# Squares of chunk 1 summed by TensorE tile by tile, and the keys of chunk 0 between the memory keys and the spread of chunk 1's norm

## The chip, the cores and the metric

One core of a Trainium2 chip runs the whole program. The metric is the device time of one execution in microseconds (us); the time of a kernel is the median of its runs. Engines are named as in the profile: PE is TensorE (its weight loads are listed as PEld), DVE is VectorE, ACT is ScalarE, POOL is GpSimd, SP is SyncE, which issues nearly all DMAs here.

## What is computed

One step of a hybrid encoder layer on 1024 prompt tokens and 32 sample tokens (1056 columns, model width 1024), all in float32. Cut to what matters here:

```python
def rmsnorm(x, g):
    x32 = x.astype(jnp.float32)
    y = x32 * lax.rsqrt(jnp.mean(x32 * x32, axis=-1, keepdims=True) + EPS)
    return (y * g.astype(jnp.float32)).astype(x.dtype)

def memory_kv(mem, g, wk, wv):
    mn = rmsnorm(mem, g)
    mk = (mn @ wk).reshape(B, M, X_HEADS, X_HEAD_DIM)
    mv = (mn @ wv).reshape(B, M, X_HEADS, X_HEAD_DIM)

q, k, v, ga, bb, cc, hh, gb, xq, gx, mg = split(rmsnorm(x, g) @ w_in)
# window attention (q, k, v), short convolution (cc, hh, bb), attention into 256 memory tokens (xq, mk, mv),
# each times its SiLU gate and projected; the three merged, projected by w_out, added to x; a last rmsnorm
```

The change lies in the head of the program: the norm of x, the memory keys and values, and the first projections (keys and values, then queries).

## The kernel before

x lies transposed, width on the partitions: two chunks of 528 columns (c = 0, 1), each in eight tiles of 128 x 528, two to a buffer (`xr`). The work of the head, for each chunk:

- ACT squares the eight tiles (`sq`, tag `gt`, three buffers); DVE adds them into the first one (`x_squares`, L461); TensorE then sums that one tile over its 128 partitions with six small matmuls against a column of ones (`csx`, L417, in `column_rstd`).
- DVE turns the sums into mean + eps (`vax`, L421), POOL raises them to the power -0.5 (`rsx`, L424).
- TensorE spreads the result over the partitions with six more matmuls (`rpx`, L428, in `r_chunk`), ACT copies that out (`Rx`, L436), and DVE multiplies the eight tiles by it (L466, `x_norm`).
- ACT and DVE split each normed piece into a high part (`xh`, `b`, L483) and a low part (`xl`, `b`, L95), the operands of all later products (`x_blocks`); `x_sums` makes further operands from sums of pieces (`kwt`, `qht`, `aot`, `vwt`, L500), which are first used by the group q2 behind the queries.

Every float32 product is three matmuls (high by high, high by low, low by high: L99, L100, L101, in `mm3`). `kv_group` makes keys and values from the operands of a chunk (`pdkv`): it is a generator, and each `next(kv)` emits the work up to its next yield. `q_direct` makes the first queries in four passes (`pdq`): weight tile 0 for chunk 0 and chunk 1, then weight tile 1 for chunk 0 and chunk 1. Its weights, too, are split by ACT (`whq`, L115) and DVE (`wlq`, L95). `mk_step(f)`, f = 0 to 3, makes the memory keys (`mkp`, L585), eight float32 matmuls each, which the trace records as two each.

Each engine runs its instructions in the order in which they stand in the program; a framework of tiles sets the semaphores, gives buffers out, and may move an instruction against the order of the code. All input loads stand in one row on SP. From the group q2 on, POOL prepares the weights of the long middle of the program (`S_q`, L131, and `wlq`, L95).

Of the kernel before, what the change touches and what calls it, by code (L numbers as in the profile page):

```python
# [33 lines left out]
def stream_kernel(tc, A, O):  # L34
# [4 lines left out]
    with ExitStack() as ctx:  # L39
# [333 lines left out]
        def kv_group(nm, f2):  # L373
# [3 lines left out]
            for c in range(2):  # L377
                for i in range(2):
                    ps = bank2(f"pd{nm}{c}{i}")
                    for s in range(2):  # L380
                        for kh in range(2):
                            hi, lo = w[2 * i + kh]
                            for k in range(4):
                                kc = slice(k * 128, (k + 1) * 128)
                                xh, xl = (x[k] for x in XD[c, kh, s])
                                mm3(ps[:, s, :H], hi[:, kc], lo[:, kc], xh, xl, kh + k == 0, kh == 1 and k == 3)
                    act.copy(o[i].rearrange("p (s c h) -> p s c h", s=2, c=2)[:, :, c], ps[:, :, :H])
                if c == 0:
                    yield
            yield  # L390
# [21 lines left out]
        def column_rstd(parts, cols, w, nm, pair_=False):  # L412

            ps = bank2(f"cs{nm}")[:, 0] if pair_ else bank(f"cs{nm}")
            for j in range(cols):
# [24 lines left out]
        def slot(c, j, l):  # L440
            return 14 * c + 2 * j + l
# [11 lines left out]
        def x_squares(c):  # L453
# [8 lines left out]
            return tot  # L462

# [433 lines left out]
        for i in range(4):  # L897
            if i < 3:
                mem_load(i + 1)
            for k in (2 * i, 2 * i + 1):  # L900
                wmv.append(mem_w(A["w_mv"][k], f"rmv{k}", ("whi", "wlo")[k // 4], 4))
                if 0 < k < 5:
                    x_load(0, k - 1, slot(1, (T1, T2)[(k - 1) // 2], (k - 1) % 2))
        for k in range(4):
            x_load(1, k, slot(1, (T4, T3)[k // 2], k % 2))
        wmk = [mem_w(A["w_mk"][k], f"rmk{k}", *(("S", 3), ("qh", 2), ("kw", 2), ("vw", 2), ("ao", 2), ("raw", 5))[max(k - 2, 0)])
               for k in range(8)]
# [4 lines left out]
        sq = [x_squares(c) for c in range(2)]  # L912
        r0 = column_rstd([sq[0]], 6, 88, "x0", True)
        MS["rs"] = column_rstd([MS["acc"][:, :256], MS["acc"][:, 256:]], 2, 128, "m", True)
        mk_step(0)
        R0 = r_chunk(r0, "x0")
        x_norm(0, R0)
        mk_step(1)
        r1 = column_rstd([sq[1]], 6, 88, "x1", True)
# [3 lines left out]
        mk_step(3)  # L923
        R1 = r_chunk(r1, "x1")
# [5 lines left out]
        x_blocks(1, [sb.tile([128, NT], F32R, name=f"b12c1{l}", tag="O", bufs=4) for l in range(2)])  # L930
        next(kv)
# [284 lines left out]
```

## Time and profile before

| | us |
|---|---|
| median of 3 runs | 1005.92 (1005.43 to 1006.57) |
| the profiled execution, its own time | 1011.11 |
| its span, first to last instruction | 1009.3 |
| PE busy in the span | 982.1 |
| DVE, ACT, POOL busy in the span | 510.7, 465.1, 561.4 |

The rows are times within the one profiled execution, counted from its first instruction. A busy engine is one with an instruction under way; what it waits for in a given stretch is read from that stretch and not from the share of the whole span.

### The profile page before, as it was taken

Reading aid. Unit: us, or ns where it says so; the run is one execution under the profiler, and the core shown is the slowest. Engines: PE = TensorE matmul, PEld = TensorE weight load, DVE = VectorE, ACT = ScalarE, POOL = GpSimd, SP = SyncE. Lnnn points to the kernel's source line nnn. Section 1 sums busy time; section 2 is a strip of 40 time slices with the busy share of each in tenths; the row PEclk is TensorE's granted clock in tenths of the full one; section 3 lists DMA queues with packets and bytes.
Section 4 is the critical chain, followed back from the end, with each engine's and each line's share of the span. In section 5 each row is a group of like instructions: output and inputs, shape, how many; then the busy total and the mean of one; then the engine's idle time right before and its main releaser. Section 6 shows DMA issues by size and latency. Waiting matters only on the chain.

```text
span 1009.3 us, 20193 instructions
## 1 busy us (share of the span) xinstructions
PE 982.1 (97%) x7887; PEld 958.1 (95%) x7887; DVE 510.7 (51%) x836; ACT 465.1 (46%) x969; POOL 561.4 (56%) x422
## 2 busy tenths in 40 slices
PE   8799999999999999999999999999999999999996
PEld 4699999999999999999999999999999999999996
DVE  3787333466575656565443333333374472552464
ACT  5454434455445454454454545545372242243452
POOL 0505677665667676767555555555554444444463
PEclk9899999999999999999999999999999999999998
DMA  9445633454423232322354444434686678653473
GB/s 338 145 150 156 204 133 110 152 170 138 128 67 103 74 112 85 99 75 86 105 161 149 154 151 148 138 120 153 210 281 201 182 201 254 183 188 88 126 233 118
DMA packets 115711, 153.06 MB, mean 152 GB/s; under 512 B 14400, under 2 KB 73888, under 8 KB 115616
## 3 DMA queue, kind: packets, MB, share of 16 engines
q1 hardware_dynamic: 115040, 151.24, 48.0%
q8 instruction: 62, 1.02, 0.4%
q10 hardware_dynamic: 576, 0.54, 0.2%
q14 instruction: 33, 0.27, 0.1%
HBM read 109.49 MB, written 42.25 MB: 150 GB/s over the span
## 4 chain that ended last, share of the span: by engine, by line
PE 85%; DVE 8%; DMA 2%; ACT 2%; POOL 2%; issue 1%; SPq 0%; POOLq 0%; DVEq 0%; ACTq 0%
PE y L99 4%; PE y L101 4%; PE y L100 4%; PE wo L99 3%; PE wo L101 3%; PE wo L100 3%; PE pamg L99 2%; PE pamg L100 2%; PE pdmg L99 2%; PE pamg L101 2%; PE pdmg L100 2%; PE pdmg L101 2%; PE pcmg L99 2%; PE pcmg L100 2%; PE pcmg L101 2%; PE mvp L550 2%
## 5 line engine op out<-in xcount | busy, mean ns | idle before, releaser
L95 POOL TENSOR_TENSOR wlp<-rp,whp 128x512 fp32r<-128x512 f32 x80 | 104.9, 1312 | 128.7 <-ACT whp L115 128.6
L115 ACT CAST whp<-rp 128x512 fp32r<-128x512 f32 x96 | 59.6, 621 | 130.3 <-PE y L100 78.7
L99 PE MATMUL y<-br,whp 128*128 128x264 f32 x384 | 109.2, 284 | 1.2 <-DVE z L271 1.2
L100 PE MATMUL y<-br,whp 128*128 128x264 f32 x384 | 109.1, 284 | 0.0
L101 PE MATMUL y<-br,wlp 128*128 128x264 f32 x384 | 109.0, 284 | 0.0
L95 POOL TENSOR_TENSOR wlmg<-S_mg,whmg 128x512 fp32r<-128x512 f32 x48 | 62.7, 1307 | 56.2 <-ACT whmg L115 42.5
L95 POOL TENSOR_TENSOR wlmg<-rmg,whmg 128x512 fp32r<-128x512 f32 x36 | 47.0, 1306 | 62.1 <-ACT whmg L115 59.3
L101 PE MATMUL wo<-zo,wlp 128*128 128x264 f32 x256 | 73.0, 285 | 0.8 <-POOL wlp L95 0.8
L99 PE MATMUL wo<-zo,whp 128*128 128x264 f32 x256 | 73.2, 286 | 0.3 <-ACT whp L115 0.3
L99 PEld LDWEIGHTS y<-br,whp 128*128 128x128 f32 x384 | 72.1, 188 | 1.3 <-ACT whp L115 1.3
L100 PE MATMUL wo<-zo,whp 128*128 128x264 f32 x256 | 72.6, 284 | 0.0
L100 PEld LDWEIGHTS y<-br,whp 128*128 128x128 f32 x384 | 72.3, 188 | 0.0
L101 PEld LDWEIGHTS y<-br,wlp 128*128 128x128 f32 x384 | 72.3, 188 | 0.0
L99 PE MATMUL pcmg<-xh,whmg 128*128 128x264 f32 x192 | 55.5, 289 | 1.2 <-DVE omg L218 1.2
L99 PE MATMUL pamg<-xh,whmg 128*128 128x264 f32 x192 | 55.3, 288 | 0.0
L99 PE MATMUL pdmg<-xh,whmg 128*128 128x264 f32 x192 | 55.2, 287 | 0.0
L100 PE MATMUL pcmg<-xl,whmg 128*128 128x264 f32 x192 | 54.7, 285 | 0.0
L100 PE MATMUL pdmg<-xl,whmg 128*128 128x264 f32 x192 | 54.7, 285 | 0.0
L100 PE MATMUL pamg<-xl,whmg 128*128 128x264 f32 x192 | 54.7, 285 | 0.0
L101 PE MATMUL pdmg<-xh,wlmg 128*128 128x264 f32 x192 | 54.6, 284 | 0.0
L101 PE MATMUL pcmg<-xh,wlmg 128*128 128x264 f32 x192 | 54.4, 284 | 0.0
L101 PE MATMUL pamg<-xh,wlmg 128*128 128x264 f32 x192 | 54.4, 283 | 0.0
(493 smaller groups left out, 3674.3 us busy)
## 6 DMA issues: line engine op xcount, KB each, us to landing
MGd<-omg SPq DMA_DIRECT2D x24, 528.0 KB, 3.6
sg<-MGd SPq DMA_DIRECT2D x48, 264.0 KB, 3.1
rmg<-in_w_in SPq DMA_DIRECT2D x48, 256.0 KB, 2.8
rp<-in_w_p SPq DMA_DIRECT2D x48, 256.0 KB, 3.1
rp<-in_w_out SPq DMA_DIRECT2D x48, 256.0 KB, 2.8
xr<-in_xT SPq DMA_DIRECT2D x8, 528.0 KB, 7.9
res<-in_xT SPq DMA_DIRECT2D x8, 528.0 KB, 5.7
qtw<-Qd SPq DMA_DIRECT2D x32, 128.0 KB, 2.6
```

What stands on the lines that cost most here:

```text
L95: eng.tensor_tensor(out=lo, in0=x, in1=hi.bitcast(F32), op=ALU.subtract)
L99: pe.matmul(out, lh, rh, start=first, stop=False, skip_group_check=free)
L100: pe.matmul(out, lh, rl, start=False, stop=False, skip_group_check=free)
L101: pe.matmul(out, ll, rh, start=False, stop=last, skip_group_check=free)
L115: act.copy(hi, src)
L550: pe.matmul(mps[m], mt(k)[:, m * 128:(m + 1) * 128], w, start=k == 0, stop=k == 7)
```

## The change

It changes four things, all in the head. Chunk 1's squares are no longer added up by DVE: a new function `x_columns` lets TensorE sum each of the eight squared tiles by itself, with six matmuls each that add into the same bank, and the main row calls it in pieces (four tiles, two tiles, two tiles) between the steps of the memory keys. The first two loads of `w_mk` are issued between the two halves of chunk 1. `kv_group` yields also after the keys of a chunk, and its first part (the keys of chunk 0) is called ahead of `r_chunk` for chunk 1. The squares of chunk 1 are called behind both statistics of chunk 0 and of the memory.

```diff
                     act.copy(o[i].rearrange("p (s c h) -> p s c h", s=2, c=2)[:, :, c], ps[:, :, :H])
-                if c == 0:
                     yield
-            yield
             move(out=O["attn_k"], in_=o[0][:, 896:1056])
...
-        def column_rstd(parts, cols, w, nm, pair_=False):
-
-            ps = bank2(f"cs{nm}")[:, 0] if pair_ else bank(f"cs{nm}")
-            for j in range(cols):
+        def column_rstd(parts, cols, w, nm, pair_=False, sums=None):
+
+            ps = sums if sums is not None else bank2(f"cs{nm}")[:, 0] if pair_ else bank(f"cs{nm}")
+            for j in range(cols if sums is None else 0):
...
+        def x_columns(c, ks, st={}):
+
+            if 0 in ks:
+                st["ps"] = bank2(f"csx{c}")[:, 0]
+            for k in ks:
+                sq_ = half("gt", f"sq{c}_{k}", F32, 3)
+                act.activation(sq_, xk(c, k), AF.Square)
+                for j in range(6):
+                    pe.matmul(st["ps"][:88, 2 * j:2 * j + 2], sq_[:, j * 88:(j + 1) * 88], one.broadcast_to([128, 2]),
+                              start=k + j == 0, stop=k == 7 and j == 5, skip_group_check=True)
+            return st["ps"]
...
         for k in range(4):
+            if k == 2:
+                wmk_load(0)
+                wmk_load(1)
             x_load(1, k, slot(1, (T4, T3)[k // 2], k % 2))
...
-        sq = [x_squares(c) for c in range(2)]
-        r0 = column_rstd([sq[0]], 6, 88, "x0", True)
+        r0 = column_rstd([x_squares(0)], 6, 88, "x0", True)
         MS["rs"] = column_rstd([MS["acc"][:, :256], MS["acc"][:, 256:]], 2, 128, "m", True)
+        x_columns(1, range(4))
         mk_step(0)
+        x_columns(1, range(4, 6))
         R0 = r_chunk(r0, "x0")
         x_norm(0, R0)
         mk_step(1)
-        r1 = column_rstd([sq[1]], 6, 88, "x1", True)
+        r1 = column_rstd(None, 6, 88, "x1", sums=x_columns(1, range(6, 8)))
         x_blocks(0, [xslot(slot(0, T4, l), f"b12{l}", F32R) for l in range(2)])
         kv = kv_group("kv", (T_K, T_V))
         mk_step(2)
         mk_step(3)
+        next(kv)
         R1 = r_chunk(r1, "x1")
         x_norm(1, R1)
         mem_spread()
...
+        next(kv)
         next(kv)
         x_sums(0)
```

What this does to the order on the engines is shown at three places. Numbers behind a name tell buffers apart and differ between the two programs. The first is PE from the column sums of chunk 0 (`csx0`) on. Before, the spread of chunk 0 (`rpx0`) follows them, then the memory keys of steps 0 and 1 (`mkp0`), and the column sums of chunk 1 (`csx1`) behind these:

```order
L417 MATMUL csx0_235<-cst_81,sq0_0_189 88x2 x6
L428 MATMUL rpx0_264<-cst_81,rsx0_244 128x88 x6
L585 MATMUL mkp0_255<-memt0_96,rmk0_136 128x256 x2
L585 MATMUL mkp0_255<-memt1_98,rmk0_136 128x256 x2
L585 MATMUL mkp0_255<-memt2_106,rmk1_138 128x256 x2
L585 MATMUL mkp0_255<-memt3_116,rmk1_138 128x256 x2
L585 MATMUL mkp0_255<-memt0_96,rmk2_140 128x256 x2
L585 MATMUL mkp0_255<-memt1_98,rmk2_140 128x256 x2
L585 MATMUL mkp0_255<-memt2_106,rmk3_142 128x256 x2
L585 MATMUL mkp0_255<-memt3_116,rmk3_142 128x256 x2
L417 MATMUL csx1_289<-cst_81,sq1_0_212 88x2 x6
```

Of the change, the same place, behind the column sums of chunk 0 and down to its spread (`mkp0` down to `rmk1` is step 0):

```order
L470 MATMUL csx1_232<-cst_81,sq1_0_233 88x2 x6
L470 MATMUL csx1_232<-cst_81,sq1_1_241 88x2 x6
L595 MATMUL mkp0_265<-memt0_96,rmk0_132 128x256
L470 MATMUL csx1_232<-cst_81,sq1_2_249 88x2 x6
L595 MATMUL mkp0_265<-memt0_96,rmk0_132 128x256
L470 MATMUL csx1_232<-cst_81,sq1_3_257 88x2 x6
L595 MATMUL mkp0_265<-memt1_98,rmk0_132 128x256 x2
L595 MATMUL mkp0_265<-memt2_106,rmk1_134 128x256 x2
L595 MATMUL mkp0_265<-memt3_116,rmk1_134 128x256 x2
L470 MATMUL csx1_232<-cst_81,sq1_4_274 88x2 x6
L470 MATMUL csx1_232<-cst_81,sq1_5_282 88x2 x6
L426 MATMUL rpx0_290<-cst_81,rsx0_221 128x88 x6
```

Six groups of column sums and the whole of step 0 now stand ahead of chunk 0's spread; the last two groups stand behind step 1. Of the keys of chunk 0 the framework puts only two matmuls ahead of chunk 1's spread; the spread is third in the row behind step 3.

The second place is DVE between `vax1` (chunk 1's mean) and the multiplications by chunk 1's norm (L466). Before, its end is:

```order
L95 TENSOR_TENSOR wlkv10_396<-rkv10_393,whkv10_395 128x512
L95 TENSOR_TENSOR wlkv11_402<-rkv11_399,whkv11_401 128x512
L500 TENSOR_TENSOR kwt00_649<-xr0_0_104 128x528
L500 TENSOR_TENSOR kwt01_650<-xr0_1_110 128x528
L500 TENSOR_TENSOR qht00_651<-xr0_2_114,kwt00_649 128x528
L500 TENSOR_TENSOR qht01_652<-xr0_3_120,kwt01_650 128x528
L95 TENSOR_TENSOR xl0_3_654<-kwt00_649,xh0_3_653 128x528
L466 SCALAR_TENSOR_TENSOR xr1_0_128<-xr1_0_128,cst_81,Rx1_348 128x528 x2
```

Of the change:

```order
L95 TENSOR_TENSOR wlkv10_391<-rkv10_388,whkv10_390 128x512
L95 TENSOR_TENSOR wlkv11_397<-rkv11_394,whkv11_396 128x512
L476 SCALAR_TENSOR_TENSOR xr1_0_128<-xr1_0_128,cst_81,Rx1_459 128x528 x2
L476 SCALAR_TENSOR_TENSOR xr1_1_130<-xr1_1_130,cst_81,Rx1_459 128x528 x2
L476 SCALAR_TENSOR_TENSOR xr1_2_136<-xr1_2_136,cst_81,Rx1_459 128x528 x2
```

The five subtractions of `x_sums` (`kwt`, `qht`, `xl0_3`) that stood ahead of chunk 1's norm now stand behind it, among the pieces of chunk 1.

The third place is DVE around `wlq010`, the low part of the weights of the queries' third pass. Before, from the last piece `xl1_4` (chunk 1) on:

```order
L95 TENSOR_TENSOR xl1_4_777<-xr1_1_130,xh1_4_776 128x528
L367 SCALAR_TENSOR_TENSOR q1q000_747<-pdq000_697,q0q000_746 128x528
L95 TENSOR_TENSOR xl1_6_783<-aot10_752,xh1_6_782 128x528
L95 TENSOR_TENSOR xl1_6_783<-aot11_753,xh1_6_782 128x528
L95 TENSOR_TENSOR wlq010_854<-rq010_851,whq010_853 128x512
```

Of the change:

```order
L367 SCALAR_TENSOR_TENSOR q1q000_782<-pdq000_732,q0q000_781 128x528
L510 TENSOR_TENSOR xr1_1_130<-xr1_3_138,xr1_1_130 128x2x264
L510 TENSOR_TENSOR aot11_788<-xr1_3_138,vwt11_790 128x528
L277 SCALAR_TENSOR_TENSOR e1kv0_881<-okv_0_400,e0kv0_880 128x528
L95 TENSOR_TENSOR xl1_4_812<-xr1_0_128,xh1_4_811 128x528
L95 TENSOR_TENSOR xl1_4_812<-xr1_1_130,xh1_4_811 128x528
L95 TENSOR_TENSOR wlq010_889<-rq010_886,whq010_888 128x512
```

Between `q1q000` (the low part of the first queries, the first instruction in a long row with only one input from SBUF, the other from PSUM) and `wlq010` there stood two instructions; now there are five. From the first L466 of chunk 1 to `wlq010` there stood 51, and now 54.

## Rows read from the trace of the kernel before

**Rows 1.** Busy time on the page: engine, us, share of span, instructions.

```profile
PE 982.1 (97%) x7887; PEld 958.1 (95%) x7887; DVE 510.7 (51%) x836; ACT 465.1 (46%) x969; POOL 561.4 (56%) x422
```

**Rows 2.** Busy time by stretch: start:end, length, engines, granted clock, DMA share, GB/s.

```profile
24.82:26.94 2.12, 0.00 (x1) 0.00 (x1) 1.88 (x5) 1.28 (x2) 1.84 (x2) 1.00 1.05 387
27.70:31.00 3.30, 3.30 (x13) 2.94 (x12) 1.14 (x2) 1.67 (x3) 0.18 (x1) 0.50 1.04 372
45.00:48.00 3.00, 0.00 (x0) 0.00 (x0) 2.76 (x5) 1.25 (x2) 3.00 (x1) 1.00 0.85 265
48.20:54.90 6.70, 5.91 (x26) 5.85 (x27) 2.38 (x4) 2.57 (x5) 0.73 (x1) 0.50 0.06 23
100.00:1009.00 909.00, 892.69 (x7345) 880.68 (x7344) 441.01 (x732) 414.03 (x879) 534.57 (x410) 1.00 0.48 147
```

**Rows 3.** Waits of PE in the first 75 us: total, times, longest.

```profile
PE rpx L428 <- POOL rsx L424: 6.1, 2, 4.0
```

**Rows 4.** Timeline of PE in the head: start, us, instruction, [idle before <- releaser].

```profile
23.79 1.03 PE L417 MATMUL csx<-cst,sq 128*88 128x2 f32 x12
26.94 2.25 PE L428 MATMUL rpx<-cst,rsx 88*128 88x88 f32 x12 [2.12 <-POOL rsx L424]
36.95 1.03 PE L417 MATMUL csx<-cst,sq 128*88 128x2 f32 x12
37.84 7.15 PE L585 MATMUL mkp<-memt,rmk 128*128 128x256 f32 x32
48.99 2.86 PE L428 MATMUL rpx<-cst,rsx 88*128 88x88 f32 x12 [4.00 <-POOL rsx L424]
...
76.98 0.28 PE L99 MATMUL pdq<-xh,whq 128*128 128x264 f32 x1
...
89.52 0.39 PE L101 MATMUL pdq<-xh,wlq 128*128 128x264 f32 x1 [0.50 <-DVE wlq L95]
```

**Rows 5.** Timeline of ACT, two places.

```profile
24.86 0.64 ACT L457 ACTIVATE sq<-xr 128x528 f32<-128x528 f32 x1 [1.66 <-PE csx L417]
...
29.23 0.60 ACT L436 COPY Rx<-rpx 128x528 f32<-128x528 f32 x1 [2.85 <-PE rpx L428]
```

**Rows 6.** Timeline of DVE, from chunk 0's norm to the queries' weights.

```profile
29.86 0.77 DVE L466 SCALAR_TENSOR_TENSOR xr<-xr,cst,Rx 128x528 f32<-128x528 f32 x1 [2.53 <-ACT Rx L436]
...
38.39 0.15 DVE L421 TENSOR_SCALAR vax<-csx 88x6 f32<-88x6 f32 x1
38.47 0.69 DVE L95 TENSOR_TENSOR xl<-xr,xh 128x528 fp32r<-128x528 f32 x1
39.08 0.70 DVE L95 TENSOR_TENSOR b<-xr,b 128x528 fp32r<-128x528 f32 x1
...
47.06 0.70 DVE L95 TENSOR_TENSOR xl<-kwt,xh 128x528 fp32r<-128x528 f32 x1
52.52 5.52 DVE L466 SCALAR_TENSOR_TENSOR xr<-xr,cst,Rx 128x528 f32<-128x528 f32 x8 [4.76 <-ACT Rx L436]
...
61.43 1.29 DVE L95 TENSOR_TENSOR mkl<-mko,mkh 128x512 fp32r<-128x512 f32 x2 [1.58 <-ACT mkh L595]
...
84.24 0.69 DVE L367 SCALAR_TENSOR_TENSOR q1q<-pdq,q0q 128x528 fp32r<-128x528 f32 x1
84.86 2.90 DVE L95 TENSOR_TENSOR xl<-aot,xh 128x528 fp32r<-128x528 f32 x2
87.69 3.47 DVE L95 TENSOR_TENSOR wlq<-rq,whq 128x512 fp32r<-128x512 f32 x2
```

**Rows 7.** Timeline of POOL, four of its first rows.

```profile
25.10 1.79 POOL L424 TENSOR_TENSOR rsx<-vax,cst 88x6 f32<-88x6 f32 x1 [24.66 <-DVE vam L421]
...
38.62 10.31 POOL L424 TENSOR_TENSOR rsx<-vax,cst 88x6 f32<-88x6 f32 x1 [10.74 <-DVE vax L421]
78.71 6.77 POOL L131 TENSOR_TENSOR S_q<-rq,rq 128x512 f32<-128x512 f32 x1 [29.77 <-DMA rq<-in_w_in]
...
90.57 1.73 POOL L95 TENSOR_TENSOR wlq<-S_q,whq 128x512 fp32r<-128x512 f32 x1
```

More of the change, by code (lines that the diff above doesn't have):

```diff
@@ L903, in stream_kernel, with wmk_load @@
                     x_load(0, k - 1, slot(1, (T1, T2)[(k - 1) // 2], (k - 1) % 2))
+        wmk = []
+        def wmk_load(k):
+            tag = (("S", 3), ("qh", 2), ("kw", 2), ("vw", 2), ("ao", 2), ("raw", 5))[max(k - 2, 0)]
+            wmk.append(mem_w(A["w_mk"][k], f"rmk{k}", *tag))
         for k in range(4):
+            if k == 2:
+                wmk_load(0)
+                wmk_load(1)
             x_load(1, k, slot(1, (T4, T3)[k // 2], k % 2))
-        wmk = [mem_w(A["w_mk"][k], f"rmk{k}", *(("S", 3), ("qh", 2), ("kw", 2), ("vw", 2), ("ao", 2), ("raw", 5))[max(k - 2, 0)])
-               for k in range(8)]
+        for k in range(2, 8):
+            wmk_load(k)
         for i in range(4):
```

## The prediction, made blind

> **What bounds the kernel now.** The page comes first: TensorE is busy for 982.1 of 1009.3 us [rows 1], so there is little to win, and what there is lies where TensorE stands still or runs slowly. The busy time by stretch shows where. From 100 us on TensorE is busy for 892.69 of 909 us at full clock, 0.12 us a matmul (892.69 by 7345) [rows 2]; nothing of the change reaches in there. In the head it stands still twice, from 24.82 to 26.94 and for 4.00 us before 48.99, both times for POOL's power `rsx`, 6.1 us together [rows 3, 4]. After each of these waits the granted clock reads 0.50, the 1.2 GHz level: from 27.70 to 31.00 and from 48.20 to 54.90, where TensorE is busy for 3.30 and 5.91 us and so loses about half of that, 4.6 us [rows 2].
>
> The timeline of TensorE shows one more thing that decides here: at 89.52 it waits 0.50 us for `wlq`, a low part of weights that VectorE makes [rows 4]. From chunk 1's norm at 52.52 until then VectorE is the engine that is late; TensorE has just so much work that it arrives half a microsecond early. Whatever makes VectorE later in that stretch is paid in full, since behind it TensorE hardly waits for anything.
>
> **The column sums on TensorE.** Six small matmuls (one group, twelve records) hold TensorE from 36.95 to 37.84: 0.89 us [rows 4]. Eight groups take the place of one: 7 x 0.89 = 6.2 us more. The seven additions that VectorE loses (about 0.7 us each, like its other two-input instructions [rows 6]) are worth nothing by themselves, because VectorE stands still for 4.76 us before chunk 1's norm anyway [rows 6].
>
> What matters is what the groups stand in front of. `csx0` ends at 23.79 + 0.89 = 24.68. Behind it now stand six groups (5.3 us) and step 0 of the memory keys, half of the 7.15 us that two steps take (3.6) [rows 4]. So the spread of chunk 0 begins at 33.6, where it began at 26.94. ACT does not hold that up further: the fourth square started at 24.86, with the end of the sums before it, and takes 0.64 us [rows 5], less than a group. The two loads put ahead of half of chunk 1 are 0.5 MB, 1.3 us at the 387 GB/s of that stretch [rows 2]; they cost nothing, since the groups that need that half stand behind step 0, after 31 us.
>
> **Chunk 1's statistic.** The spread, ACT's copy and the way to VectorE took 3.53 us for chunk 1 (48.99 to 52.52, of it 2.86 us of matmuls at the low clock) and 2.92 us for chunk 0 [rows 4 to 6]. With TensorE busy before it I take the full clock, 3.53 - 1.4 = 2.1 us: chunk 0's norm begins at 35.7. Eight multiplications take 5.5 us [rows 6], and `vax` of chunk 1 stands behind them: 41.2, against 38.39 before. The last column sums are done by then (33.6 + 1.4 of spread + 3.6 of step 1 + 1.8 of two groups = 40.4).
>
> Then POOL's power. Before, it was issued at 38.62 and took 10.31 us [rows 7]. Meanwhile VectorE ran fifteen instructions without a gap, all with two inputs from SBUF, from 38.47 to 47.76, and POOL ended 1.17 us after the last [rows 6, 7]. So I read it as shut out while that row lasts. The change takes three of the fifteen out (twelve are left: eight low parts and four of weights, as the order on VectorE shows), 0.62 us each by the starts at 38.47 and 39.08: 10.54 - 1.9 = 8.7 us from `vax`, so `rsx` is there at 49.9, against 48.93. TensorE is through with steps 2 and 3 at 47.6 and waits 2.3 us instead of 4.0. The two matmuls of chunk 0's keys ahead of the spread fill 0.24 us, and the other 46 are queued behind the waiting spread: yielding the keys earlier buys next to nothing. After so short a wait (2.12 us before 26.94) chunk 0's way took 2.92 us; I take that. VectorE begins chunk 1's norm at 52.8, against 52.52: **+0.3 us**.
>
> The Trainium skill has a rule that speaks against my reading of that row. Its page "SBUF — State Buffer", section "SBUF: two separate sides", calls the ports that VectorE and GpSimd share an exclusive lock that the one that starts first holds for its whole instruction. By that, POOL would wait for one instruction of 0.7 us and not for fifteen, and `rsx` would be there before TensorE needs it, which makes my sum 2.3 us smaller; the 10.31 us of the trace do not look like it.
>
> **VectorE from chunk 1's norm to `wlq010`.** Before: 52.52 to about 89.4. Three instructions more stand between them (five subtractions come in, two pieces `xl1_6` go behind): 3 x 0.62 = **+1.9 us**. Then POOL again. Its first `S_q` was issued at 78.71 and took 6.77 us: it came through with `q1q` at 84.24, which reads only one input from SBUF [rows 6, 7]. From there on POOL and VectorE hold each other up: the two `xl` take 2.90 us and the two `wlq` 3.47 us, 1.7 us a piece in place of 0.62, until POOL's five instructions end at 92.30 [rows 6, 7]. Of the five VectorE instructions held up so, three were on the way to `wlq010` (0.5, 1.1 and 1.1 us). Now `q1q` has five ahead of `wlq010` behind it: all five, 4.9 us in place of 2.7, **+2.2 us**. What bounds it: 0 if POOL came late, 2.7 less if VectorE is never held up. VectorE's gap of 1.58 us [rows 6] changes its cause: `mko` now waits for the spread of the memory's norm, which stands behind 60 matmuls of keys and values (7.2 us, up to 1.7 more at the low clock). That gap is 0.6 to 2.3 us by this; I take no difference (-1.0 to +0.7).
>
> So `wlq010` comes 0.3 + 1.9 + 2.2 = 4.4 us later, at about 93.8. TensorE had 40.0 us of work between 48.99 and 89.02, up to 3 us of them lost to the clock [rows 2, 4], and is there at 87 to 90. It waits 4 to 7 us.
>
> **The clock behind that wait.** Nothing of before shows this place; nearest are the waits of 2.12 and 4.00 us, both followed by a granted 0.50, for at least 3.30 us of work [rows 2]. Bounds 0 and 3.0; by the shorter row half of 3.3, **+1.7 us**.
>
> **Sum.** 4.4 + 1.7 = +6.1 us. The profiled execution took 1011.11 us for a span of 1009.3, and is 5.2 us above the median of the runs; I add to the median: 1005.92 + 6.1 = **1012.0 us** (a span of about 1015 if the profile again falls that high).
>
> **Rivals.**
> *The low clock in the column sums.* In place of the first wait TensorE gets groups of matmuls with two columns. If these do as little for the clock as the wait did, step 0 and the groups up to the spread run at 0.50 from 27.6 on, up to 5.9 us of work twice as long. For it: the clock fell there before. Against: the lone group at 36.95 left it alone. I take half, 3 us, all of it on chunk 1's statistic: 1015.0.
> *POOL is not shut out.* If the power comes through after one VectorE instruction, the spread waits only for TensorE's own row (47.6), 2.3 us earlier; and if POOL's first `S_q` likewise starts when it is issued, its five are over before `wlq010` matters and the 2.2 and the 1.7 us fall away: 0.3 - 2.3 + 1.9 = -0.1, 1005.8. Against it stand both long rows of POOL (10.31 and 6.77 us); for it the first `rsx`, 1.79 us beside running additions [rows 7]. The rule of the skill gives this one.
> *TensorE gets its idle time back.* If VectorE's chain is no bound, 6.6 us of waits and 4.6 us of low clock are to be had for 6.2 us of column sums: at best -5.0, 1000.9; with one wait left (2.3 us, and its clock) about 1004. It decides when `wlq010` is there before 89, so VectorE would have to save 5 us of my sum.
>
> **How the numbers follow.** My forecast 0.55, the low clock in the sums 0.13, POOL not shut out 0.20, idle time given back 0.12. A measurement of this kernel can tell about 0.2%, 2 us, from no change. Faster: the last case, 0.12. Same: the third, 0.20 (the forecast at its lowest, 0.3 + 1.9 alone, is still just beyond 2 us). Slower: the rest, 0.68. The range goes from 1004, the third case with a little gain, to 1015.5, where the second is half left out; the forecast's own range is 1008 to 1015.
>
> **What the profile after would show.** `rpx` of chunk 0 at 33 to 34 and `vax` of chunk 1 at about 41; a `rsx` of 8 to 9 us on POOL and a wait of about 2 us for it; five slowed VectorE instructions behind `q1q` and a wait of TensorE of over 4 us for `wlq`; a granted 0.50 behind that. I am wrong if `rsx` takes about 1 us, if `wlq010` is there when TensorE is, or if the granted clock is 0.50 from 27 to 35.

## The result, and the profile after

The change makes the kernel slower: 1018.53 us (1017.55 to 1020.39, 4 runs) against 1005.67 (1005.11 to 1006.57), a ratio of 1.0127 (95% interval 1.0095 to 1.0159), +12.9 us. Forecast were +6.1 and 1012.0; the sign was right, the size was not, and the time lies outside the range.

Busy time on the page of the changed kernel; [rows 1] answers to it:

```profile
PE 990.7 (97%) x7971; PEld 965.5 (95%) x7971; DVE 505.6 (50%) x829; ACT 464.6 (46%) x969; POOL 547.2 (54%) x422
```

TensorE has 84 more records (42 matmuls, seven groups of sums) and 8.6 us more of busy time, where 6.2 us were forecast. That difference does not show the loss in the head, since the head before also had a part at the low clock (4.6 us lost, [rows 2]). Its stretches after the change do (start:end, length, busy time of the five engines, granted clock, DMA share, GB/s):

```profile
24.85:28.50 3.65, 3.65 (x40) 3.54 (x41) 0.00 (x0) 1.76 (x4) 1.93 (x2) 1.00 1.05 388
28.60:35.30 6.70, 6.70 (x25) 5.57 (x24) 0.00 (x0) 1.05 (x2) 0.00 (x0) 0.50 0.43 146
38.90:42.10 3.20, 3.20 (x9) 2.57 (x9) 2.52 (x4) 1.64 (x3) 0.00 (x0) 0.50 0.00 0
42.30:52.90 10.60, 10.60 (x67) 9.54 (x66) 9.71 (x18) 5.38 (x10) 1.72 (x1) 1.00 0.01 3
```

TensorE never stands still here, and yet 9.9 us of it run at 0.50, about 5 us lost. Its timeline shows the same in the instructions (start, length, idle before in brackets):

```profile
24.85 2.01 PE L470 MATMUL csx<-cst,sq 128*88 128x2 f32 x24 [0.34 <-DVE vam L419]
...
28.74 1.82 PE L470 MATMUL csx<-cst,sq 128*88 128x2 f32 x12
30.42 5.27 PE L595 MATMUL mkp<-memt,rmk 128*128 128x256 f32 x12
...
37.36 1.55 PE L426 MATMUL rpx<-cst,rsx 88*128 88x88 f32 x12
38.74 5.34 PE L595 MATMUL mkp<-memt,rmk 128*128 128x256 f32 x16
...
45.75 7.15 PE L595 MATMUL mkp<-memt,rmk 128*128 128x256 f32 x32
...
52.98 1.47 PE L426 MATMUL rpx<-cst,rsx 88*128 88x88 f32 x12
```

A group (12 records) takes 1.8 us at 28.74 and about half of that at 24.85. The spread of chunk 0 comes at 37.36 (forecast 33.6, before 26.94 [rows 4]); that of chunk 1 waits for nothing but TensorE's own row. VectorE and POOL:

```profile
39.58 5.52 DVE L476 SCALAR_TENSOR_TENSOR xr<-xr,cst,Rx 128x528 f32<-128x528 f32 x8 [14.81 <-ACT Rx L434]
46.00 0.16 DVE L419 TENSOR_SCALAR vax<-csx 88x6 f32<-88x6 f32 x1 [0.90 <-PE csx L470]
55.12 5.52 DVE L476 SCALAR_TENSOR_TENSOR xr<-xr,cst,Rx 128x528 f32<-128x528 f32 x8 [1.61 <-ACT Rx L434]
```

```profile
46.24 1.72 POOL L422 TENSOR_TENSOR rsx<-vax,cst 88x6 f32<-88x6 f32 x1 [19.46 <-DVE vax L419]
```

POOL's power for chunk 1 takes 1.72 us, where 8.7 were forecast and 10.31 stood before [rows 7], although VectorE again runs its row of subtractions right beside it. TensorE's waits show the wait for `wlq` as forecast, at 93.51 and 96.42, and two late ones, before the scores against the memory (`Sxs`) and before the last projection (`wo`); given are total, times and longest:

```profile
PE pdq L101 <- DVE wlq L95: 3.1, 2, 1.9
PE Sxs L99 <- ACT ckhxs L846: 2.6, 1, 2.6
PE wo L99 <- ACT whp L115: 2.0, 1, 2.0
```

### The profile page after: what moved, and what is told of

It is laid out like the page before. It is cut to its first block, busy times and chain, and to the rows that moved or that the text cites. A ratio compares the mean times of both kernels' runs of the same rounds, so it can differ in the third digit from the quotient of the medians.

```text
span 1018.2 us, 20355 instructions
## 1 busy us (share of the span) xinstructions
PE 990.7 (97%) x7971; PEld 965.5 (95%) x7971; DVE 505.6 (50%) x829; ACT 464.6 (46%) x969; POOL 547.2 (54%) x422
## 4 chain that ended last, share of the span: by engine, by line
PE 87%; DVE 7%; DMA 2%; ACT 2%; issue 1%; POOL 0%; SPq 0%; POOLq 0%; ACTq 0%; DVEq 0%
PE y L99 4%; PE y L101 4%; PE y L100 4%; PE wo L99 3%; PE wo L101 3%; PE wo L100 3%; PE pamg L99 2%; PE pdmg L99 2%; PE pdmg L100 2%; PE pdmg L101 2%; PE pamg L100 2%; PE pamg L101 2%; PE pcmg L99 2%; PE pcmg L100 2%; PE pcmg L101 2%; PE mkp L595 2%
```

## The experiments

The kernel before ran again beside each of five groups of experiments; its medians there were 1004.68, 1005.70, 1005.41, 1007.64 and 1006.35 us. A ratio is to the runs of the kernel before in the same group. A profile is of one execution; where that one lies far from the median of its kernel, the text says so.

**A second profile of both kernels.** No edit.

> The kernel before, unchanged, for a second profile: its first profiled execution took 1011.1 us, 5.4 above the median of its runs. If the excess lies in the head, this profile (at about 1005.7, a span near 1004) shows less of the two waits for the power (6.1 us together in the first profile) or of the granted 0.50 behind them (27.6 to 31.0 and 48.1 to 54.9). If it lies late, the head is the same to 0.5 us and 3 to 5 us are missing behind 100 us, at a wait or a stretch at 0.50 that only the first profile has. Time: 1005.7 within 0.2% by either.

Measured: 1005.43 us at the median of ten runs, the profiled one at 1010.38. Of the 107 runs of the kernel before in these groups, the ten included, 71 lie between 1002.9 and 1007.7 and 36 between 1009.7 and 1014.4, none in between: it has two kinds of executions, some 6 us apart, and both of its profiles are of the rarer, longer one. The head repeats, with 6.1 us of waits for the power again. VectorE and then POOL in that second profile:

```profile
37.87 0.16 DVE L421 TENSOR_SCALAR vax<-csx 88x6 f32<-88x6 f32 x1
37.94 0.70 DVE L95 TENSOR_TENSOR xl<-xr,xh 128x528 fp32r<-128x528 f32 x1
```

```profile
38.10 10.31 POOL L424 TENSOR_TENSOR rsx<-vax,cst 88x6 f32<-88x6 f32 x1 [10.75 <-DVE vax L421]
```

> The changed kernel, unchanged, for a second profile. Theory: the head repeats within 0.5 us (0.50 in the column sums from 28 on, the spread of chunk 0 at 36 to 37.5, chunk 1's norm near 55, a wait for wlq of 1.5 to 2.5 us), since POOL's power is not shut out there and nothing else in it is left to chance. Of the two late waits (2.59 us before the scores against the memory at 706, 2.01 us before the last projection at 981) I expect both again, within 1 us; if they are chance, at least one is below 1 us. Time 1016 to 1020.

Measured: 1021.39 us (1019.09 to 1022.49), ratio 1.0148 (1.0125 to 1.0171). Here the power takes 8.45 us and TensorE waits 2.3 us for it, nearly what I had forecast (8.7 and 2.3):

```profile
45.48 8.45 POOL L422 TENSOR_TENSOR rsx<-vax,cst 88x6 f32<-88x6 f32 x1 [18.44 <-DVE vax L419]
```

So the power of the changed kernel, too, is short in one execution and long in another, and my expectation that nothing in its head is left to chance was wrong. The wait before the last projection came again (1.7 us), the one before the scores at 1.5 us only.

**The parts.** The sums without the new yields and loads (the squares of chunk 1 stay behind the two statistics), and the yields alone. The edit of the yields, without its second `next(kv)` behind the pieces of chunk 1:

```diff
-                if c == 0:
                     yield
-            yield
...
         mk_step(3)
+        next(kv)
         R1 = r_chunk(r1, "x1")
```

> The kernel before with chunk 1's squares summed tile by tile on TensorE, in the places that the change gives them; the loads and the yields of the keys stay as they were. Theory one (the column sums run at a granted 0.50 and set the head): nearly all of the +12.9 us is here, 1016 to 1019, with 0.50 in the sums between 28 and 42 us, the spread of chunk 0 at 35 to 37 and of chunk 1 without a wait behind TensorE's own row at about 52.5. Rival (the new order of the keys and of VectorE's pieces behind chunk 1's norm makes the weights wlq late): the sums alone give at most half, 1006 to 1011.

> The kernel before with the yields of the keys changed and the first keys called ahead of the spread of chunk 1; sums and loads as before. Theory one: nothing measurable, 1004 to 1007, since the spread is still waited for (4 us before 49) with two matmuls of the keys ahead of it at most. Rival (the order of the pieces makes wlq late): 1008 to 1012, with a wait of TensorE of 2 us or more for wlq near 90 to 95 us.

Measured: the sums alone 1016.36 us, ratio 1.0113 (1.0083 to 1.0143); the yields alone 1006.71, ratio 1.0027 (1.0003 to 1.0051). The sums bring nearly all of it; the loads were not run alone. The profile of the yields alone is the first of the shorter kind; VectorE and POOL in it:

```profile
38.70 0.16 DVE L419 TENSOR_SCALAR vax<-csx 88x6 f32<-88x6 f32 x1 [0.32 <-PE csx L415]
38.79 0.69 DVE L95 TENSOR_TENSOR xl<-xr,xh 128x528 fp32r<-128x528 f32 x1
```

```profile
38.95 1.72 POOL L422 TENSOR_TENSOR rsx<-vax,cst 88x6 f32<-88x6 f32 x1 [10.47 <-DVE vax L419]
```

The same instructions stand at the same distances as in the longer kind (the subtraction 0.16 us ahead of the power, the next one behind it). What differs in these rows is that VectorE had waited for the column sums ahead of `vax`. Four of the eleven runs of the yields alone lie at 1009.5 to 1014.4, so the longer kind did not go with them.

**The clock.** The sums as two matmuls of 256 columns a tile, with about the same time on TensorE. Ones are now loaded and the squares moved, and the sums come out over other columns than the norm needs, so only the time is read:

```diff
-                for j in range(6):
-                    pe.matmul(st["ps"][:88, 2 * j:2 * j + 2], sq_[:, j * 88:(j + 1) * 88], one.broadcast_to([128, 2]),
+                for j in range(2):
+                    pe.matmul(st["ps"][:88, 256 * j:256 * j + 256], one.broadcast_to([128, 88]), sq_[:, 256 * j:256 * j + 256],
...
```

> The changed kernel with each group of six matmuls of 2 columns (a column of ones moved, the squares loaded as weights) turned into two of 256 columns (ones loaded, the squares moved): about the same 0.89 us a tile at full clock by the memory keys' 0.45 us each. The sums so made are not those that the norm needs (it reads sums of other columns), so only the time counts. Theory one: the granted clock stays at 1.00 from 27 to 42 us, the spread of chunk 0 starts at about 33.6 as forecast, the power for chunk 1 does not hold TensorE up, chunk 1's norm starts near 50 in place of 55.1, and the time is 4 to 6 us below the change, 1012 to 1015. Rival (what is late is VectorE's chain to wlq, whatever the clock): the head is earlier up to chunk 1's norm, but the waits for wlq grow by as much and less than 2 us is won, 1016.5 to 1018.5. A second rival (the clock falls there whatever runs): 0.50 again between 28 and 42, and no gain.

Measured: 1013.78 us, ratio 1.0078 (1.0048 to 1.0108). The clock held, but in the profile the power took 14.66 us (no wait of VectorE ahead of `vax`) and brought a wait of 3.1 us:

```profile
42.64 14.66 POOL L422 TENSOR_TENSOR rsx<-vax,cst 88x6 f32<-88x6 f32 x1 [14.56 <-DVE vax L419]
```

The rest of this group therefore has the power held; how is told next.

> The kernel with the wide column sums (not those of the reference: only the time counts) and the small VectorE instruction that waits for the power. The clock should stay at 1.00 through the whole head. Theory one (the clock in the sums and what comes of it is most of the loss; 6.2 us of sums less the 2.1 us wait and 1.7 us of low clock that before has is +2.4 us): the spread of chunk 1 without a wait at 54 or earlier, and 1007 to 1010 at the median. Rival (VectorE's later order makes wlq late): a wait of 2 us or more for wlq near 90 us, 1010 to 1013.

Measured: 1009.65 us, ratio 1.0037 (1.0013 to 1.0061), no wait for `wlq`. In the stretches of its head up to 54 us the clock is 1.00 throughout:

```profile
24.20:34.20 10.00, 9.97 (x52) 8.21 (x53) 0.69 (x1) 4.09 (x7) 1.96 (x2) 1.00 0.73 264
34.20:54.00 19.80, 19.80 (x122) 18.02 (x121) 17.74 (x30) 10.12 (x18) 1.71 (x1) 1.00 0.21 68
```

Against the held changed kernel (1017.90, below) this is 8.2 us: the narrow shape of the sums is two thirds of the loss. It is not all clock. By the starts of equal matmuls the heads of the two profiles are 8.7 us apart at 100 us, some 5 of it time at 0.50 and 3.0 waits for `wlq`. The wait before the last projection, told below, adds about 2 us in the held changed kernel. On the other side this profile is of the slowest of ten runs, 3.4 us above their median, and it has a loss of 4.3 us that the profile of the held changed kernel has not: up to 111.65 TensorE waits 2.90 us for VectorE (`u2q`), with a 0.50 of 3.4 us behind it.

Next, the spread of chunk 0 ahead of the sums:

```diff
-        x_columns(1, range(4))
-        mk_step(0)
-        x_columns(1, range(4, 6))
         R0 = r_chunk(r0, "x0")
         x_norm(0, R0)
+        x_columns(1, range(4))
+        mk_step(0)
+        x_columns(1, range(4, 6))
```

> The changed kernel with the held power for chunk 1 and the spread of chunk 0 ahead of the column sums of chunk 1 (two matmuls of the memory keys stay ahead of it). Theory one (TensorE's row of sums at the low clock bounds the head up to the keys, whatever stands in front of what): 0.50 in the sums again, TensorE at the keys of chunk 0 at about 52, but chunk 0's norm some 10 us earlier than 39.6, so that VectorE's chain is early and the waits for wlq (3.0 us) go: 1013 to 1016, 2 to 4 us less than the held change at 1017.9. Rival (the place in front of the spread is most of the loss): 1006 to 1011. Second rival (the place makes no difference): 1017 to 1020.

Measured: 1017.77 us (1016.41 to 1022.49), ratio 1.0101 (1.0043 to 1.0159). Chunk 0's norm begins at 29.60 and the waits for `wlq` are gone, as expected, but 0.50 stands from 29.7 to 36.4 and the median is that of the held change. With four runs each, whose ranges overlap, a gain of the 2 to 4 us that I expected is neither shown nor excluded; that the place in front of the spread is most of the loss is ruled out.

Then the true sums two tiles at a time between the steps of the memory keys; the spread and the pieces of chunk 0 (`x_blocks`) move with them:

```diff
-        x_columns(1, range(4))
-        mk_step(0)
-        x_columns(1, range(4, 6))
+        x_columns(1, range(2))
         R0 = r_chunk(r0, "x0")
         x_norm(0, R0)
+        mk_step(0)
+        x_columns(1, range(2, 4))
         mk_step(1)
+        x_columns(1, range(4, 6))
+        x_blocks(0, [xslot(slot(0, T4, l), f"b12{l}", F32R) for l in range(2)])
+        mk_step(2)
         r1 = column_rstd(None, 6, 88, "x1", sums=x_columns(1, range(6, 8)))
...
```

> The changed kernel with the held power, the spread of chunk 0 behind two tiles of sums, and the other sums two tiles at a time between the steps of the memory keys (true sums, narrow matmuls). Theory one (bunched narrow sums lower the clock; a lone group did not): the granted clock stays at 1.00 or has one stretch of 0.50 between 27 and 45 us, the spread of chunk 0 at about 27, the first keys at 47 to 49, no wait for wlq above 1 us, 1006 to 1010. Rival (any narrow sums lower it, spaced or not): two or more stretches at 0.50 and 1013 to 1018.

Measured: 1013.88 us (1011.96 to 1017.29), ratio 1.0053 (1.0023 to 1.0083). My expectation fell: spacing does not save the clock (6.6 us at 0.50, in place of 9.9):

```profile
30.10:33.40 3.30, 3.30 (x9) 2.59 (x9) 3.15 (x5) 2.14 (x5) 0.00 (x0) 0.50 0.45 141
36.90:40.20 3.30, 3.30 (x8) 2.60 (x9) 3.30 (x7) 2.66 (x5) 0.00 (x0) 0.50 0.00 0
```

The median is 4 us below that of the held change, but not shown to be so by the clock: the spread ahead of the sums had as little time at 0.50 and no gain in its median, and this profile is of the slowest of the ten runs (1017.29).

**POOL and VectorE.** First try: six small VectorE instructions with their one input from PSUM, which the framework puts between the subtractions behind `vax`.

```diff
+            if nm == "x1":
+                vb = sm.tile([128, 6], F32, name="vb", tag="vb")
+                for _ in range(6):
+                    dve.tensor_scalar(out=vb[:w, :cols].unsqueeze(2), in0=pv_[:, :, 0:1], scalar1=1.0 / D, scalar2=EPS,
+                                      op0=ALU.mult, op1=ALU.add)
```

> The kernel before with six small VectorE instructions behind the mean of chunk 1 that repeat it into a spare tile; each has one input, from PSUM, and the framework puts them between the subtractions that follow. Theory (two kinds of executions of the kernel before: in those near 1010.5 POOL's power for chunk 1 is shut out by VectorE's row and takes 10.3 us, in those near 1004.5 it is not; both profiles of before are of the first kind, the medians of the second): the power takes under 3 us, the spread of chunk 1 follows TensorE's own row at about 45 us without a wait, no 0.50 behind it, no wait for wlq near 89; all runs lie within 1003 to 1007, none at 1010 or above, the median 1004 to 1005.5. Rival (the second kind of execution comes from elsewhere): the power is short, but runs at 1010 and above appear as often as before (about 7 in 31), or the median falls by 3 us or more.

> The kernel with the wide column sums and the six small VectorE instructions that let POOL in; as there the sums are not those of the reference, so only the time counts. In the wide kernel the clock stayed at 1.00 through the sums, but the power for chunk 1 took 14.66 us and cost a wait of 3.1 us and a stretch at 0.50 (6.8 us). With POOL let in: no wait for the power, chunk 1's norm at about 55 (TensorE's own row to 54, the spread 1.5 us), 3.1 + 3.4 = 6.5 us less up to there; theory one (TensorE's row is the bound of the head): 1007 to 1010 at the median. Rival (VectorE's chain to wlq is the bound behind it): a wait of TensorE of 2 us or more for wlq near 88 us, and 1010 to 1014.

> The kernel before with the six small VectorE instructions, and the first two loads of the memory keys' weights ahead of half of chunk 1, as the change has them; with these there in time the framework puts step 0 of the memory keys ahead of the spread of chunk 0. TensorE then has 3.6 us of work where it waits 2.1 us for the first power and runs 3.3 us at 0.50 after it. Theory one (the head is bound by TensorE): 2.1 + 1.7 us less than the kernel with the small instructions alone, 1000 to 1002.5. Rival (what the spread of chunk 0 loses, 1.5 us, delays VectorE and comes back as a wait for chunk 1's norm or wlq): 1003 to 1006.

All three missed: 1012.68, 1016.06 and 1010.57 us (ratios 1.0070, 1.0098, 1.0043). The small instructions let POOL in nowhere: the power took 10.12, 15.08 and 6.47 us, and every run of the first was of the longer kind (1010.8 to 1015.6). In the third the framework also moved the weights `wlkv` behind chunk 1's norm, and TensorE waited 6.1 us for them.

Second try: one VectorE instruction that reads the power.

```diff
             pool.tensor_tensor(out=rs[:w, :cols], in0=va[:w, :cols], in1=nhalf[:w].broadcast_to([w, cols]), op=ALU.pow)
+            if nm == "x1":
+                vb = sm.tile([128, 6], F32, name="vb", tag="vb")
+                dve.tensor_scalar(out=vb[:w, :cols], in0=rs[:w, :cols], scalar1=1.0, scalar2=0.0, op0=ALU.mult, op1=ALU.add)
```

> The kernel before with one small VectorE instruction that reads POOL's power for chunk 1, one subtraction behind the mean: VectorE stands still until the power is there, so no row of its instructions can shut POOL out. (The six small instructions before did not let POOL in; it took 10.1 us there.) Theory (the median of before comes from executions in which the power is not shut out): the power takes under 2.5 us, no wait of TensorE for the spread of chunk 1, no 0.50 from 48 on, chunk 1's norm at 48 to 50.5 in place of 52.5, no wait for wlq near 89; every run within 1003 to 1008, median 1004 to 1006, none of 1009 and above. Rival (the kind of execution is decided elsewhere): the power is short, and runs of 1010 still appear, or the median moves by more than 2 us from before.

> The changed kernel with the same small VectorE instruction behind chunk 1's mean. In its first profile the power took 1.72 us and nothing waited, in the second 8.45 us and TensorE waited 2.3 us, with a stretch at 0.50 behind it. With POOL always let in I expect the first kind in every run: 1017 to 1020, the power under 2.5 us, 0.50 in the column sums, a wait for wlq of 2 to 4 us near 95. If the spread of the changed kernel's runs (1017.5 to 1022.5) comes from the power, the runs lie within 2.5 us. Rival: VectorE's 1 us of standing still comes back at wlq and the time is 1 us above that.

Measured: before, held: 1006.10 us, twelve runs from 1004.94 to 1008.79, ratio 1.0008 (0.9988 to 1.0028). Changed, held: 1017.90 (1015.76 to 1020.88), ratio 1.0119 (1.0081 to 1.0156). With POOL let in, the longer kind of the kernel before did not come (11 of the 29 runs beside it were of that kind). VectorE in the first:

```profile
37.84 0.16 DVE L421 TENSOR_SCALAR vax<-csx 88x6 f32<-88x6 f32 x1 [0.33 <-PE csx L417]
37.92 0.69 DVE L95 TENSOR_TENSOR xl<-xr,xh 128x528 fp32r<-128x528 f32 x1
39.83 0.17 DVE L427 TENSOR_SCALAR vb<-rsx 88x6 f32<-88x6 f32 x1 [1.21 <-POOL rsx L424]
...
48.50 2.12 DVE L469 SCALAR_TENSOR_TENSOR xr<-xr,cst,Rx 128x528 f32<-128x528 f32 x3
```

Chunk 1's norm begins at 48.50, 4 us earlier than in [rows 6], even though VectorE stood still for 1.21 us. The times say that the kernel before typically does the same, though none of its own shorter executions was profiled. VectorE had waited for the sums here too; but in the wide held and in the held and filled kernel it had not, and the power took 1.71 us with the reading instruction there as well. The changed kernel's runs still spread over 5 us, so the power is not what spreads them.

Does the wait ahead of `vax` decide? The column sums of chunk 1 made twice, so that VectorE always waits, alone and with eight unread matmuls behind `csx0` in the first wait:

```diff
-            for j in range(cols):
+            for j in list(range(cols)) * (2 if nm == "x1" else 1):
...
+        fps = bank("fps")
+        for i in range(8):
+            pe.matmul(fps[:, 0:128], sq[0][:, 0:128], sq[0][:, 128:256], start=True, stop=True)
```

> The kernel before with the six column sums of chunk 1 made twice (the second time over the first, same result): TensorE is done with them 0.9 us later, so VectorE, which reached the mean 0.3 us early or a little late before, always waits for them. Theory (the power is let in where VectorE has waited just before the mean): the power takes under 2.5 us in the profile, every run lies within 1003.5 to 1008, none at 1009.5 or above, median 1004.5 to 1006. Rival (which of the two kinds comes is chance that has nothing to do with this wait): about a third of the runs at 1010 or above, as before (18 of 60 so far at 1010 and above).

> The kernel of the held power, and eight matmuls of 128 columns behind the column sums of chunk 0, whose result nobody reads: 1.9 us of work in TensorE's wait of 2.1 us for the first power. Theory (the granted 0.50 of 3.3 us that follows that wait comes of the wait): 1.00 from 27 to 33 us, and 1.5 to 2 us less than the kernel of the held power alone, 1002.5 to 1004. Rival (VectorE bounds the stretch behind, so what TensorE saves becomes a wait): within 0.7 us of it.

> The kernel with the doubled column sums of chunk 1 and the eight unread matmuls in TensorE's wait for the first power. There is no wait of VectorE for POOL as in the filled kernel before (it stood still for 1.2 us and TensorE then waited 2.4 us for wlq). Theory: 1.00 from 27 us on, the power let in, a wait for wlq of about 1 us, 1003 to 1005 with no run above 1008: this would be the steadiest version, and as fast as the good runs of before. Rival (the power is shut out in a part of the runs since VectorE no longer waits for the sums): runs 5 us or more above the others.

Measured: doubled 1006.41 us, ratio 0.9989 (0.9964 to 1.0015), the power 1.72 us in the profile, but two of twelve runs at 1010.8 and 1012.1, and two more at 1008.6 and 1009.2, between the two kinds of before. Against the 36 in 107 of before, twelve runs can't tell that from no effect, and it is not none as I expected: the wait goes with being let in, it was not shown to bring it. Held and filled 1006.37 us, ratio 0.9990 (0.9966 to 1.0014): the stretch at 0.50 behind the first power is gone, and what TensorE saves turns into a wait of 2.4 us for `wlq` with a 0.50 of its own behind it, the rival. Doubled and filled 1005.74 (1002.55 to 1008.07), ratio 0.9974 (0.9954 to 0.9995), again 2.4 us for `wlq`: about the time of the shorter kind of before without the longer one, and the only version here that is measurably ahead of the runs beside it (of those 11 of 23 were of the longer kind).

**The late waits.** Unread matmuls of two columns at the very start, 42 for the kernel of the held power and 32 for the wide one with the held power, bring both to the changed kernel's 7971 records:

```diff
             pe.matmul(wps[:, 0:128], warm[:, 128:256], warm[:, 128:256], start=True, stop=True)
+        for i in range(42):
+            pe.matmul(wps[:, 0:2], warm[:, 128:256], warm[:, 128:130], start=True, stop=True)
```

> The kernel of the held power with 42 unread matmuls of two columns more at the very start, where TensorE has about 2 us to wait for the first data: as many more instructions of TensorE as the narrow column sums bring, none of them in the place of the sums. What it loses at the start (2 to 5 us) doesn't matter; looked at are the two late waits. Theory (the number of instructions brings them): the wait before the scores near 700 is 1.9 us or more and the one before the last projection 1.5 us or more. Rival (lateness of the head or the sums' own place brings them): 1.6 and 0.3 us or less, as in the kernel of the held power.

> The kernel of the wide column sums and the held power with 32 unread matmuls of two columns at the start, which bring TensorE's instructions to the number of the changed kernel; only the time counts, since the sums are of other columns. Theory (the number of instructions brings the late waits): 1.9 us or more near 700 and 1.5 us or more near 975, where the kernel without the padding shows 1.6 and under 0.3. Rival: as there.

Measured (1025.41 and 1022.84 us; the padding delays the start more than I thought, in the first by some 15 us). TensorE's waits in the padded kernel of the held power:

```profile
PE wo L101 <- ACT whp L117: 2.1, 1, 2.1
```

That wait was 0.2 us without the padding; in the wide kernel it rose from under 0.2 to 0.8. Over all profiles it is 1.7 to 2.1 us in seven of the eight with 7971 records (the eighth is the padded wide one) and 0.5 or less in all twelve with 7887 to 7915. The wait before the scores did not move (1.7 and 1.8), so half of what I expected came. The padded kernels start late, but lateness alone does not bring the wait before the last projection: by the starts of equal matmuls the wide kernel comes there 8.9 us later than the held kernel before and waits 0.2 us, the sums alone come 7.6 us later and wait 1.9.

The padding itself shows the clock once more. In the padded wide kernel TensorE does nothing but these matmuls of two columns from 4.61 to 15.0, without a gap, and the clock falls among them:

```profile
5.40:8.70 3.30, 3.30 (x32) 3.30 (x31) 0.69 (x1) 2.38 (x5) 0.00 (x0) 1.00 1.01 366
8.90:15.00 6.10, 6.10 (x30) 6.10 (x30) 0.71 (x1) 1.14 (x2) 0.00 (x0) 0.50 1.03 406
```

They load other operands than the column sums and share with them only that two columns are moved. In the other padded kernel the 84 records take 17.92 us, 0.21 each, the pace of the second row here; hence the late start.

## Why the prediction was wrong, step by step

**The step that failed first: "I add to the median".** The sum was made against a profile that took 1011.11 us, and was added to a median of 1005.92. These are different kinds of executions. In the kind of the profile POOL's power is shut out, and the change takes most of that loss away (TensorE waits 4.0 us for that power before, 2.3 us in one profile of the change and not at all in the other); the median has no such loss, as far as the held kernel before shows it in its place. There chunk 1's norm begins at 48.50, and in the changed kernel at 55.12: +6.6 us, where I had +0.3 (against the profile's 52.52 it is +2.6). Of the 6.8 us by which the median missed, 3.2 lie between the two profiled times (1020.39 - 1011.11 = 9.3, forecast 6.1), and 5.4 come from the profile before standing above its median, less 1.9 by which the profile after stands above its own. The sign was in my hands: the profiled time lay 5.2 us above the median, and above the slowest, of the runs shown.

Against the profile itself the forecast was nearer: a span of about 1015, measured 1018.2. By the starts of equal matmuls the head ended 5.2 us later than in that profile (forecast 6.1), which is partly luck: chunk 1's norm came 2.3 us later than forecast and a second wait for `wlq` of 1.2 us was not in the sum, while VectorE's way from the norm to `wlq010` was 2.7 us shorter and the 0.50 behind the wait, 1.7 us, did not come. The late waits bring the rest.

**The column sums.** "Seven more groups, 6.2 us" was right for groups at full clock (a group took about 0.9 us at 24.85). That the low clock would stay away from them was not; it was a rival with chance 0.13 and half of 5.9 us. It came over 9.9 us, and chunk 0's norm began at 39.58 (forecast 35.7). With wide matmuls of about the same time it did not come, and the held time fell by 8.2 us, not all of it by the clock.

**Chunk 1's statistic.** "POOL is shut out by the row" (8.7 us) came true in one of two profiles of the changed kernel (8.45 us), and not in the other (1.72 us). The rival that it is not shut out had 0.20; it did not occur to me that one kernel does both. The Trainium skill's page "SBUF — State Buffer", section "SBUF: two separate sides", has the one that starts first hold the shared ports for its whole instruction. The short rows of this power agree with that, the long ones do not. With VectorE idle the power takes 1.33 us, as for chunk 0 in the changed kernel:

```profile
24.79 1.33 POOL L422 TENSOR_TENSOR rsx<-vax,cst 88x6 f32<-88x6 f32 x1 [24.34 <-DVE vam L419]
```

Issued 0.16 us behind the start of a subtraction, it takes 1.72 and ends 1.18 us behind the end of that one subtraction (46.08 + 0.69 and 46.24 + 1.72 in the changed kernel); the subtractions that follow keep their 0.70. Where it takes 10.31, 8.45 or 14.66 us it ends 1.18 us behind the end of the last instruction of the row (47.06 + 0.70 and 38.62 + 10.31 in [rows 6, 7]). So it waits either for the one instruction that runs when it is issued, as the rival had it, or for the whole row.

**VectorE to `wlq010`.** It begins at 92.77, takes 0.68 and is there at 93.45 (forecast 93.8, from a start of the norm 2.3 us too early). VectorE's gap for `mko`, which I left as it was, shrank from 1.58 to 0.31 us. A wait came there as forecast: 3.1 us in two (forecast 4 to 7, and a 0.50 behind it, which did not come). `q1q` was followed by three slowed instructions and not five, since POOL paused for 2.98 us.

**Where the +12.9 us lie.** Against the profile of the held kernel before (span 1004.9) the changed one is 13.3 us longer. By the starts of equal matmuls it is 4.6 us behind in the first keys at 52 to 56 us. That is 6.2 of sums and 5.0 of low clock, less the two waits of 2.1 and 1.4 us and two stretches of 3.3 us at 0.50 that the other has, 3.3: together 4.4. The rows of that kernel:

```profile
PE rpx L431 <- POOL rsx L424: 2.1, 1, 2.1
PE pdkv L99 <- ACT Rx L439: 1.4, 1, 1.4
```

```profile
28.20:31.50 3.30, 3.30 (x10) 2.55 (x9) 2.60 (x4) 2.82 (x5) 0.00 (x0) 0.50 0.97 339
48.70:52.00 3.30, 3.30 (x17) 3.30 (x17) 3.30 (x6) 1.80 (x4) 0.00 (x0) 0.50 0.20 77
```

By 90 us it is 9.4, of which the waits for `wlq` make 2.6 (3.1 against 0.5); keys that wait for `b12c` and queries that wait for `okv` make 0.8, and the remaining 1.4 is in the order of the rows, not followed further. It stays at 9.1 to 9.4 until 690. Then come 2.5 at the scores near 700 (wait and 3.4 us at 0.50) and 1.8 at the last projection. Of the three profiles of the changed kernel, plain and held, two have the 0.50 at the scores.

**What stays open.** Why the number of TensorE's instructions moves the last projection's wait. Why POOL is let in at one time and not at another (below). Why the wait before the scores varies from 0.6 to 2.6 us. Why the changed kernel's runs spread over 5 us.

## What to carry to other kernels

Before a sum is made, lay the profiled execution's time beside all runs: if it stands 0.5% above them, ask which row of it belongs to that execution only, since a change can remove a loss that the typical run does not have. An instruction's busy time at full clock is not its price: matmuls of two columns kept TensorE busy without a gap and still took the clock from the wide ones behind them. A small instruction on POOL that the bound engine waits for should not depend on slipping in beside a row of VectorE; one VectorE instruction that reads its result cost 1.2 us of VectorE's time and left none of 24 runs of two kernels at 1009 us or above, where the kernel before has 36 of 107.

## What the runs showed of the hardware

Narrow column sums were followed by a granted 0.50, the 1.2 GHz level, in all six profiles that had all eight groups on TensorE, bunched or spaced; in the changed kernel TensorE had been busy without a gap from 24.85 us on. Wide ones of about the same time were not. Unread matmuls of two columns at the start of the padded wide kernel ran at 1.00 from 5.4 to 8.7 us and at 0.50 from 8.9, without a wait.

POOL's power of 88 x 6 takes 1.33 us with VectorE idle. Issued beside two-input instructions of VectorE, it ends 1.18 to 1.19 us behind the end of what it waits for, in all 20 profiles: the one instruction that is running (1.71 to 1.79 us in all) or, shut out, a whole row (6.47 to 15.08).

POOL's power was let in (1.72 us) in five of five profiles in which VectorE had waited 0.32 to 6.27 us for the sums just before the mean, and shut out in four of four in which it had not, where the next subtraction stood directly behind the mean. With six small PSUM instructions between, it was shut out in all three, one of them with such a wait. This is a pattern of twelve profiles; the two runs of the doubled kernel above 1010, not profiled, may speak against it. With the instruction that reads the power, it was let in in all eight profiles, three of them without such a wait.

The wait before the last projection, more than 900 us behind the column sums, went with the number of TensorE's instructions in 19 of 20 profiles.
